# An encoder trunk's MLP: up projection as seven block products, weight sums on GpSimd, down products added to the residual

## The chip, the cores and the metric

The kernel runs on one core of a Trainium2 chip. The metric is the device time of one execution in microseconds (us); of several runs the median is given. Five engines work beside each other, each on its own queue of instructions in a fixed order: TensorE (PE in the profile; its weight loads are shown apart as PEld), VectorE (DVE), ScalarE (ACT), GpSimd (POOL) and SyncE (SP), which here issues the loads of weights. TensorE reads from SBUF and writes to PSUM; all other engines work element by element. A tile framework puts the instructions in order and inserts the waits.

## What is computed

Two layers over 512 tokens of width 1024, in float32. Each layer has three mixing branches, then an MLP of width 4096:

```python
for l in range(DEPTH):
    ...                                  # three branches, gates, w_out
    x = x + merged @ w_out[l]
    hn = rms_norm(x, ln2[l])
    x = x + jnp.square(jax.nn.relu(hn @ w_up[l])) @ w_down[l]
return rms_norm(x, final_norm)
```

The MLP is where the change lies: `w_up[l]` is 1024 x 4096, `w_down[l]` 4096 x 1024. The row scale of the norm, r, is left out ahead of the MLP and comes in behind it as r squared, since relu and square let it pass.

## The kernel before

**Precision.** Every large product is made of three matmuls on a rounded high part and the rest, the low part: high x high, high x low, low x high. Weights arrive in chunks of 128x1024 (512 KB). `wsplit` (L205) makes the two parts of a chunk: ScalarE casts the high part `wh` (L207), DVE subtracts to get the low part `wl` (L208). There are three buffers of each (WB). `split` (L259) does the same with activations, on ScalarE (L262) and DVE (L263).

**Stages of a layer.** The G stage (tiles tA to gC) makes most of the input projection, then come the branches, then `yA`, `wo` (output projection into the residual `xr`, eight tiles of 128 tokens x 512), then the MLP. `norm_tok` (L306) turns `xr` for the next projection: transposes on TensorE, scale on ScalarE, low part on DVE.

**MLP.** It goes by four quarters (`qd`) of the 4096 hidden columns. In each, eight up projections (`proj`, L216, called at L1166): a chunk holds a block of 128 hidden columns over all 1024 inputs, and 8 x 3 matmuls with 512 tokens moving fill one bank of PSUM (L212 to L214). ScalarE applies relu and square (L1171, L1172). `left_first` and `left_second` (L358, L366) make block sums and differences of the result (`sf`) and their two parts (`sh`).

**Seven products.** The down projection multiplies 2x2 blocks with seven products in place of eight. `seven` (L407) does that: it needs sums of the four weight blocks b11, b12, b22, b21. `early_sums` (L400) makes t1 = b11 + b12 and then b12 + b22; two more are made ahead of product 6 and product 4 (L431, L433). All four sorts are DVE additions of 128x1024, two chunks each. Products are taken in the order 1, 2, 6, 7, 5, 4, 3; each has 24 matmuls of 512 columns and its result is added in `on`: in the first three quarters into eight tiles `acc` (copied by ScalarE where they are first written, L466, added by DVE, L468), in the last quarter scaled by r squared (`r2`, `nr2`) into `xr` (L462), after `acc` itself was added there (L473). `done` then writes `xr` to DRAM (`xspill`) or finishes the output.

**Order.** The framework orders each engine's queue; `hp()` marks urgent instructions. Weight chunks are loaded into ten buffers `wq` (NQ) for the seven products, or two buffers `wr` (WR) for the rest. GpSimd issues the loads and stores of intermediate values through DRAM, and does a few small operations.

## Time and profile before

| | us |
|---|---|
| median of 3 runs (lowest, highest) | 1730.45 (1729.51, 1731.83) |
| span of the profiled execution | 1729.5 |
| PE busy | 1685.3 |
| PEld busy | 1405.0 |
| DVE busy | 1297.1 |
| ACT busy | 1017.1 |
| POOL busy | 146.1 |

The profile gives the span from the first to the last instruction of one execution; that execution's own time is not listed apart from the three runs. Rows of groups read: line, engine, operation, tiles written and read, shapes, count, then busy us and mean ns of one, then the idle time in front. Rows by stretch give, for each engine, the busy us and the number of instructions. Rows in order of time give start and duration in us; `x2` marks two in a row, merged. The two MLPs run from about 528.6 to 861 us and from 1386.8 to 1724 us.

### The profile page before, as it was taken

The page shows a single profiled execution, that of the slowest core. Times are in us where ns is not written, and L with a number is a line of the kernel's source. Part 1 is how long each engine was busy: PE and PEld are TensorE (multiplying, and loading weights), DVE is VectorE, ACT ScalarE, POOL GpSimd, SP SyncE. Part 2 cuts the span into 40 slices and gives each one's busy share as a digit, 9 for nine tenths or more (in the row PEclk, how much of TensorE's full clock was granted, in tenths as well). Part 3 has the DMA queues.
Part 4 walks back from the last instruction along what each step waited for, and adds up shares of the span by engine and source line. Part 5 has one row for each costly group of instructions (what it writes and reads, how often), then busy time and mean ns, then how long its engine had stood idle before and what let it go on. Part 6 is the DMA issues. An engine that isn't in the chain of part 4 may idle for free.

```text
span 1729.5 us, 21976 instructions
## 1 busy us (share of the span) xinstructions
PE 1685.3 (97%) x8024; PEld 1405.0 (81%) x8024; DVE 1297.1 (75%) x2009; ACT 1017.1 (59%) x1715; POOL 146.1 (8%) x215
## 2 busy tenths in 40 slices
PE   8999999999999999999999999999999999999997
PEld 7888878887877888888888787888877878888886
DVE  7996977687566668686889869876776567686867
ACT  7665567677335555545665754877772355545454
POOL 0011200000310000000010112000004000000001
PEclk9999999999999999999999999999999999999999
DMA  8342232231545332233423422322317353232311
GB/s 331 98 146 92 83 104 81 72 104 55 203 187 182 98 110 98 98 98 98 134 92 126 147 93 71 104 79 75 111 48 273 130 182 98 98 98 97 119 65 49
DMA packets 58283, 200.04 MB, mean 116 GB/s; under 512 B 7904, under 2 KB 8288, under 8 KB 58176
## 3 DMA queue, kind: packets, MB, share of 16 engines
q1 hardware_dynamic: 44640, 154.72, 26.6%
q0 software_dynamic: 13248, 43.40, 6.7%
q8 instruction: 63, 1.03, 0.3%
q10 hardware_dynamic: 288, 0.52, 0.1%
q14 instruction: 44, 0.36, 0.1%
HBM read 177.64 MB, written 20.97 MB: 115 GB/s over the span
## 4 chain that ended last, share of the span: by engine, by line
PE 43%; issue 20%; DVE 4%; ACT 2%; POOL 0%; POOLq 0%; ACTq 0%; DVEq 0%
PE up L213 3%; PE up L212 3%; PE up L214 3%; PE dA L418 2%; PE dA L420 2%; PE dA L419 2%; PE at L558 1%; PE gA L418 1%; PE gz L214 1%; PE gz L213 1%; PE gz L212 1%; PE dC L418 1%; PE dC L420 1%; PE dC L419 1%; PE gA L420 1%
## 5 line engine op out<-in xcount | busy, mean ns | idle before, releaser
L207 ACT CAST wh<-wq 128x1024 fp32r<-128x1024 f32 x201 | 211.4, 1052 | 208.2 <-PE up L213 49.3
L208 DVE TENSOR_TENSOR wl<-wq,wh 128x1024 fp32r<-128x1024 f32 x201 | 245.1, 1222 | 117.1 <-ACT wh L207 116.1
L208 DVE TENSOR_TENSOR wl<-wr,wh 128x1024 fp32r<-128x1024 f32 x166 | 203.9, 1228 | 148.0 <-ACT wh L207 147.6
L207 ACT CAST wh<-wr 128x1024 fp32r<-128x1024 f32 x166 | 174.0, 1049 | 214.6 <-PE up L213 67.3
L212 PE MATMUL up<-xh,wh 128*128 128x512 f32 x512 | 199.2, 390 | 1.9 <-ACT u L1171 1.9
L213 PE MATMUL up<-xl,wh 128*128 128x512 f32 x512 | 200.6, 392 | 0.1
L214 PE MATMUL up<-xh,wl 128*128 128x512 f32 x512 | 199.1, 391 | 0.0
L212 PEld LDWEIGHTS up<-xh,wh 128*128 128x128 f32 x512 | 96.3, 188 | 22.7 <-ACT u L1171 2.7
L213 PEld LDWEIGHTS up<-xl,wh 128*128 128x128 f32 x512 | 96.4, 188 | 20.3 <-DVE xl L266 0.6
L214 PEld LDWEIGHTS up<-xh,wl 128*128 128x128 f32 x512 | 96.5, 189 | 19.8
L418 PE MATMUL dA<-wh,sh 128*128 128x512 f32 x256 | 99.8, 390 | 0.0
L419 PE MATMUL dA<-wh,sh 128*128 128x512 f32 x256 | 99.7, 389 | 0.0
L420 PE MATMUL dA<-wl,sh 128*128 128x512 f32 x256 | 92.6, 390 | 0.0
L600 DVE TENSOR_TENSOR ex<-ex 128x512 f32<-128x512 f32 x112 | 78.1, 715 | 6.3 <-ACT kt L575 5.4
L558 PEld LDWEIGHTS at<-qt,kt 128*128 128x128 f32 x448 | 57.0, 191 | 9.9 <-ACT kt L575 4.7
L558 PE MATMUL at<-qt,kt 128*128 128x128 f32 x448 | 59.6, 276 | 5.6 <-DVE qt L573 2.7
L572 ACT ACTIVATE qt<-ex 128x512 f32<-128x512 f32 x56 | 37.7, 674 | 46.3 <-DVE ex L600 38.5
L274 POOL TENSOR_TENSOR rs<-ms,mhalf_t 128x4 f32<-128x4 f32 (+2 forms) x15 | 17.3, 1156 | 530.6 <-DVE ms L272 527.5
L420 PEld LDWEIGHTS dA<-wl,sh 128*128 128x128 f32 x256 | 48.1, 188 | 10.0
L418 PEld LDWEIGHTS dA<-wh,sh 128*128 128x128 f32 x256 | 48.1, 188 | 10.0
L419 PEld LDWEIGHTS dA<-wh,sh 128*128 128x128 f32 x256 | 48.1, 188 | 9.9
L262 ACT CAST sh<-sf 128x512 fp32r<-128x512 f32 x64 | 39.7, 621 | 24.3 <-DVE sf L383 18.0
(403 smaller groups left out, 4403.0 us busy)
## 6 DMA issues: line engine op xcount, KB each, us to landing
wr<-in_ws_dram SPq DMA_DIRECT2D x166, 512.0 KB, 3.3
wq<-in_ws_dram SPq DMA_DIRECT2D x117, 512.0 KB, 4.3
thd<-zt POOLq DMA_DIRECT2D x32, 256.0 KB, 2.5
th<-thd POOLq DMA_DIRECT2D x32, 256.0 KB, 4.6
mgd<-mg POOLq DMA_DIRECT2D x16, 256.0 KB, 2.9
mcd<-th POOLq DMA_DIRECT2D x16, 256.0 KB, 2.5
mC<-mcd POOLq DMA_DIRECT2D x16, 256.0 KB, 6.7
mB<-mgd POOLq DMA_DIRECT2D x16, 256.0 KB, 6.6
```

What stands on the lines that cost most here:

```text
L207: nc.scalar.copy(hi, raw)
L208: nc.vector.tensor_tensor(lo, raw, hi.bitcast(F32), ALU.subtract)
L212: nc.tensor.matmul(pt, whi, xhi, start=first, stop=False)
L213: nc.tensor.matmul(pt, whi, xlo, start=False, stop=False)
L214: nc.tensor.matmul(pt, wlo, xhi, start=False, stop=last)
L262: nc.scalar.copy(hi, src)
L418: nc.tensor.matmul(pt, xh[:, t], hi[:, c], start=start and k == 0, stop=False, skip_group_check=True)
L419: nc.tensor.matmul(pt, xl[:, t], hi[:, c], start=False, stop=False, skip_group_check=True)
L420: nc.tensor.matmul(pt, xh[:, t], lo[:, c], start=False, stop=k == 3, skip_group_check=True)
L558: nc.tensor.matmul(pt[:, c], kk(st), qq[:, c], start=True, stop=True)
L572: nc.scalar.activation(qt.rearrange(shp, b=nb, h=2), e_q, AF.Exp)
L600: nc.vector.tensor_tensor(o_ap, o_ap, ap_of(ex, i_, [[istep, 2]] + z), ALU.add)
```

## The change

Four things are changed together.

The up projection is made of seven block products too. `up_unit` does half a quarter: 512 hidden columns in four 256-wide block columns and rows, over 512 tokens in two halves, so 256 tokens move in each matmul and a product has 24 matmuls. Its left side, the sums of the normed activations, is made once a layer in `norm_move` (`turn` and `sums`, with `left_sums`). Its result comes out already in the blocks that the down projection needs, and the parts for down are made product by product. `left_first` and `left_second` are gone.

The four sorts of weight sums are made by GpSimd (`eng`) in the up and the down projection, and `early_sums` there also in the G stage, except at a layer's first `uload`.

The down products of all four quarters are scaled and added straight to `xr`; `acc` is gone.

Buffers: eleven `wq`, 26 `h`, `sf` in another pool, and a scratch of 4096 bytes for the DMAs that GpSimd issues.

```diff
         for qd in range(4):
-            res += [(l, "up", qd, f) for f in range(8)]
+            res += [(l, "up", qd, j, q) for j in range(2) for q in range(4)]
...
-             "h": 22}
+             "h": 26}
...
-    WR, WB, NZ, NCT, NSM, NQ = 2, 3, 3, 4, 3, 10
+    WR, WB, NZ, NCT, NSM, NQ = 2, 3, 3, 4, 3, 11
...
+    def upload(l, qd, j):
+        first = (qd, j) == (0, 0)
+        raw = [None] * 4
+        for q in (0, 3, 1, 2) if first else range(4):
+            raw[q] = [WRAW() if first and q in (0, 3) else WQ()]
+            with hp():
+                nc.sync.dma_start(raw[q][0], ws[CHUNK[(l, "up", qd, j, q)]])
+        return raw + [[WQ() if first else WRAW()]]
...
-    def early_sums(raw):
+    def early_sums(raw, eng):
         b11, b12, b22, b21, t1 = raw
-        for i in range(2):
-            nc.vector.tensor_tensor(t1[i], b11[i], b12[i], ALU.add)
...
+        for i in range(len(t1)):
+            eng.tensor_tensor(t1[i], b11[i], b12[i], ALU.add)
+        for i in range(len(t1)):
+            eng.tensor_tensor(b12[i], b12[i], b22[i], ALU.add)
...
                     if n == 6:
-                        V.tensor_tensor(b11[i], t1[i], b22[i], ALU.add)
+                        (eng or V).tensor_tensor(b11[i], t1[i], b22[i], ALU.add)
                     elif n == 4:
-                        V.tensor_tensor(b21[i], b21[i], b11[i], ALU.add)
+                        (eng or V).tensor_tensor(b21[i], b21[i], b11[i], ALU.add)
...
+    def up_unit(raw, hx, new):
+        b11, t3, b22, b21, t1 = [t[0] for t in raw]
...
+        use = {1: ("m", b11), 2: ("a", b21), 6: ("m", b11), 7: ("s", t3), 5: ("m", t1), 4: ("s", b21), 3: ("m", b22)}
...
+            if n == 1:
+                A.copy(a11, v)
+            elif n == 2:
+                V.tensor_tensor(a11, a11, v, ALU.add)
+                square(a11)
+                put(1, a11)
+            elif n == 6:
+                A.copy(a21, v)
+            elif n == 7:
+                A.activation(a22, v, AF.Copy, scale=-1.0)
+            elif n == 5:
+                V.tensor_tensor(a22, a22, v, ALU.subtract)
+                square(a22)
+                put(4, a22)
+            elif n == 4:
+                V.tensor_tensor(a21, a21, v, ALU.add)
+                square(a21)
+                sa0, sa1 = SF(), SF()
+                V.tensor_tensor(sa0, a22, a21, ALU.subtract)
+                V.scalar_tensor_tensor(sa1, sa0, -1.0, a11, ALU.mult, ALU.subtract)
+                put(6, sa1)
+                put(5, sa0)
+                sb0 = SF()
+                V.tensor_tensor(sb0, a11, a21, ALU.subtract)
+                put(7, sb0)
...
+            else:
+                A.activation(a12, v, AF.Relu, scale=-1.0)
+                A.activation(a12, a12, AF.Square)
+                put(2, a12)
+                sb1 = SF()
+                V.scalar_tensor_tensor(sb1, a12, -1.0, h.pop("s"), ALU.mult, ALU.subtract)
+                put(3, sb1)
+        for n in (1, 2, 6, 7, 5, 4, 3):
...
+                if n == 6:
+                    G.tensor_tensor(b11, t1, b22, ALU.add)
+                elif n == 4:
+                    G.tensor_tensor(b21, b21, b11, ALU.add)
+                hi, lo = wsplit(w)
+            for f in range(2):
+                o = pt[:, f * HT:(f + 1) * HT]
+                for k in range(4):
+                    c = slice(k * HT + f * P, k * HT + (f + 1) * P)
+                    xh, xl = hx[k][n]
+                    nc.tensor.matmul(o, hi[:, c], xh, start=start and f == 0 and k == 0, stop=False, skip_group_check=True)
+                    nc.tensor.matmul(o, hi[:, c], xl, start=False, stop=False, skip_group_check=True)
+                    nc.tensor.matmul(o, lo[:, c], xh, start=False, stop=k == 3, skip_group_check=True)
...
-    def down(qd, raw, hs, acc, xr, r2, nr2, done, last):
+    def down(qd, raw, hs, xr, r2, nr2, done, last):
...
+            r = r2 if sign > 0 else nr2
+            V.scalar_tensor_tensor(xr[t][fl], pt, r[:, t:t + 1], xr[t][fl], ALU.mult, ALU.add)
...
+        seven(raw, hs, "d", on, apart=last and qd == 3, eng=nc.gpsimd)
...
-                early_sums(nxt)
+                early_sums(nxt, nc.gpsimd)
...
-        n2 = norm_tok("ln2", l, xr, False)
+        n2 = norm_move(l, xr)
...
             with hp():
-                n2.turn(fl, range(4), "s" if fl else "c")
+                n2.turn(fl)
         with hp():
             n2.end()
+            n2.sums()
...
+        raw = upload(l, 0, 0)
+        early_sums(raw, nc.gpsimd)
         for qd in range(4):
...
+            for j in range(2):
+                nxt = upload(l, qd, 1) if j == 0 else uload(l, "dn", qd, t1=WRAW)
+                hs += up_unit(raw, n2.hx, new)
+                early_sums(nxt, nc.gpsimd)
+                raw = nxt
...
+            else:
+                nxt = upload(l, qd + 1, 0)
+            down(qd, raw, hs, xr, r2, nr2, done, last)
...
-    nc = _bacc.Bacc("TRN2", target_bir_lowering=False, num_devices=1)
+    nc = _bacc.Bacc("TRN2", target_bir_lowering=False, num_devices=1, dynamic_dma_scratch_size=4096)
```

In `norm_move`, `turn` transposes `xr` as before, copies and scales it on ScalarE into `xf` (kept in float32), and makes the two parts; `sums` calls `left_sums` for four pairs of these tiles: four DVE operations of 256 columns and two splits of 512 each.

How the instructions stand shows three places. First, DVE where layer 0 goes from `wo` to the MLP, before: behind the last additions to `xr` (L1108) come the norm (L339, L272, with L1115 waiting for GpSimd's power), then weight sums of the first down projection (L403) and low parts of the turned tiles (L266).

```order
L1108 SCALAR_TENSOR_TENSOR xr_4442<-wo_4675,xr_4442 128x512
L208 TENSOR_TENSOR wl_4980<-wr_4977,wh_4979 128x1024
L339 TENSOR_TENSOR s_1062_4844<-ss_981_4451 128x4
L272 TENSOR_SCALAR ms_4846<-s_1062_4844 128x4
L1115 TENSOR_TENSOR r_1065_4850<-rs_4848 128x4
L1117 TENSOR_SCALAR r_1066_4852<-r_1065_4850 128x4
L403 TENSOR_TENSOR wq_4919<-wq_4903,wq_4907 128x1024
L266 SCALAR_TENSOR_TENSOR xl_4809<-xT_4810,vec_t,xh_4808 128x512
```

And now, on the same engine from the same place: the sums of the activations (`sf`, `xs`) stand between the norm and the low part for product 6 (`wl_5020`); of the four tiles the first and the last are shown in part.

```order
L1220 TENSOR_TENSOR r_1093_4918<-rs_4860 128x4
L1222 TENSOR_SCALAR r_1094_4920<-r_1093_4918 128x4
L383 TENSOR_TENSOR sf_4864<-xf_4817,xf_4641 128x256
L384 SCALAR_TENSOR_TENSOR sf_4864<-sf_4864,xf_4641 128x256
L387 SCALAR_TENSOR_TENSOR sf_4862<-xf_4817,sf_4864 128x256
L279 TENSOR_TENSOR xl_4820<-xf_4817,xh_4819 128x512
...
L279 TENSOR_TENSOR sh_5015<-u_4930,sh_5014 128x512
L279 TENSOR_TENSOR xs_4910<-sf_4906,xs_4909 128x512
L279 TENSOR_TENSOR xs_4915<-sf_4904,xs_4914 128x512
L224 TENSOR_TENSOR wl_5020<-wr_4932,wh_5019 128x1024
```

The low part of product 6's weight is now the thirtieth instruction behind the norm's last.

Second, GpSimd from the same norm on, before: behind the power (L274) it has nothing but the stores of the residual, which come in the last quarter.

```order
L1075 DMA mB_4547<-mgd 128x512
L1075 DMA mB_4559<-mgd 128x512
L274 TENSOR_TENSOR rs_4848<-ms_4846,mhalf_t 128x4
L1147 DMA xspill<-xr_4435 128x512
L1147 DMA xspill<-xr_4437 128x512
```

And now, further on in the same stretch, from the down sums of the first quarter (L432, L434 in `seven`) into those of the second quarter's two units (L404, L406 in `early_sums`, L551, L553 in `up_unit`):

```order
L432 TENSOR_TENSOR wq_5205<-wr_5221,wq_5213 128x1024
L432 TENSOR_TENSOR wq_5207<-wr_5222,wq_5215 128x1024
L434 TENSOR_TENSOR wq_5217<-wq_5217,wq_5205 128x1024
L434 TENSOR_TENSOR wq_5219<-wq_5219,wq_5207 128x1024
L404 TENSOR_TENSOR wr_5486<-wq_5478,wq_5480 128x1024
L404 TENSOR_TENSOR wr_5745<-wq_5737,wq_5739 128x1024
L406 TENSOR_TENSOR wq_5480<-wq_5480,wq_5482 128x1024
L406 TENSOR_TENSOR wq_5739<-wq_5739,wq_5741 128x1024
L551 TENSOR_TENSOR wq_5478<-wr_5486,wq_5482 128x1024
L553 TENSOR_TENSOR wq_5484<-wq_5484,wq_5478 128x1024
```

64 sums of 128x1024 stand in that queue in each MLP; a unit's sums stand behind the first sum of the unit after it.

Third, DVE inside the up projection of the second quarter, before: low parts of weights (L208), and sums and low parts of the results (L382 to L386, L263).

```order
L382 TENSOR_TENSOR sf_5583<-u_4862 128x256
L383 SCALAR_TENSOR_TENSOR sf_5583<-sf_5583,u_4862 128x256
L263 TENSOR_TENSOR sh_5580<-u_4862,sh_5579 128x512
L386 SCALAR_TENSOR_TENSOR sf_5544<-u_4862,sf_5583 128x256
L263 TENSOR_TENSOR sh_5587<-sf_5583,sh_5586 128x512
L263 TENSOR_TENSOR sh_5592<-sf_5544,sh_5591 128x512
L208 TENSOR_TENSOR wl_5727<-wr_5724,wh_5726 128x1024
```

And now, on the same engine: the additions from PSUM (L512, L520, L524) stand between low parts of weights (L224) that belong to later products.

```order
L512 TENSOR_TENSOR u_4930<-u_4930,up_5776 128x2x256
L224 TENSOR_TENSOR wl_5873<-wr_5486,wh_5872 128x1024
L279 TENSOR_TENSOR sh_5809<-u_4930,sh_5808 128x512
L224 TENSOR_TENSOR wl_5909<-wq_5484,wh_5908 128x1024
L224 TENSOR_TENSOR wl_5958<-wq_5482,wh_5957 128x1024
L520 TENSOR_TENSOR u_4930<-u_4930,up_5746 128x2x256
L224 TENSOR_TENSOR wl_6019<-wq_5737,wh_6018 128x1024
L524 TENSOR_TENSOR u_4930<-u_4930,up_5842 128x2x256
```

DVE's reading of product 5 (L520) now stands behind the weights of the unit's last two products.

More of the change, by code (lines that the diff above doesn't have):

```diff
@@ L398, in left_x, with seven @@
         return res
[L400 removed]
+    def early_sums(raw, eng):
         b11, b12, b22, b21, t1 = raw
[L402 to L407 removed]
+        for i in range(len(t1)):
+            eng.tensor_tensor(t1[i], b11[i], b12[i], ALU.add)
+        for i in range(len(t1)):
+            eng.tensor_tensor(b12[i], b12[i], b22[i], ALU.add)
+    def seven(raw, hs, name, on, order=(1, 2, 6, 7, 5, 4, 3), between=None, apart=False, eng=None):
         b11, t3, b22, b21, t1 = raw
@@ L1126, in trunk @@
         n1 = norm_tok("ln1", l + 1, xr, True)
-        acc = [[T("tv", "acc"), T("tv", "acc")] for _ in range(4)]
         fn_t = []
@@ L1185, in trunk @@
                     nxt = uload(l + 1, "un", 0)
-            down(qd, raw, hs, acc, xr, r2, nr2, done, last)
+            else:
+                nxt = upload(l, qd + 1, 0)
+            down(qd, raw, hs, xr, r2, nr2, done, last)
+            if qd < 3:
+                early_sums(nxt, nc.gpsimd)
+                raw = nxt
         if not last:
@@ L1190, in trunk @@
             raw = nxt
-            early_sums(raw)
+            early_sums(raw, nc.vector)
             end("mlp")
```

134 lines of the change are left out of this document (73 added, 61 removed).

## The prediction

> **What bounds the kernel now.** I read the page's first part, then busy time by stretch for one quarter of the MLP (up projection, then down), then the instructions of TensorE in order of time.
>
> ```profile
> span 1729.5 us, 21976 instructions
> PE 1685.3 (97%) x8024; PEld 1405.0 (81%) x8024; DVE 1297.1 (75%) x2009; ACT 1017.1 (59%) x1715; POOL 146.1 (8%) x215
> ...
> core 0: us, PE busy (x) PEld busy (x) DVE busy (x) ACT busy (x) POOL busy (x), PEclk, DMA share, GB/s
> 616.20:659.80 43.60, 43.60 (x194) 36.13 (x193) 24.92 (x37) 24.11 (x37) 0.00 (x0) 1.00 0.28 95
> 659.80:697.80 38.00, 38.00 (x170) 31.47 (x169) 32.90 (x38) 17.66 (x19) 0.00 (x0) 1.00 0.35 113
> ```
>
> TensorE never rests in a quarter: 43.6 us up, 38.0 us down, 81.6 us together, at full clock. DVE is busy for 57.8 of the 81.6 us, GpSimd not at all. So before the change only TensorE work counts, and DVE has 24 us per quarter to spare. Eight quarters (four in each layer) make 653 us of the span. The span is within 0.1 us of the fastest of the three runs (1729.51), so nothing worth counting lies around it; their median, 1730.45, is 1.0 above.
>
> **The matmuls.** What does one matmul cost in a stream, with 512 columns moving and with 256?
>
> ```profile
> 528.58 0.39 PE L212 MATMUL up<-xh,wh 128*128 128x512 f32 x1
> 528.81 0.39 PE L213 MATMUL up<-xl,wh 128*128 128x512 f32 x1
> 529.03 0.39 PE L214 MATMUL up<-xh,wl 128*128 128x512 f32 x1
> ...
> 1276.79 0.28 PE L964 MATMUL sc<-kl,q 128*128 128x256 f32 x1
> 1276.91 0.39 PE L254 MATMUL yC<-wh,yh 128*128 128x512 f32 x1
> ...
> 1276.67 0.19 PEld L964 LDWEIGHTS sc<-kl,q 128*128 128x128 f32 x1
> 1276.79 0.19 PEld L254 LDWEIGHTS yC<-wh,yh 128*128 128x128 f32 x1
> ```
>
> Durations (0.39) overlap; the cost is from start to start: 0.227 us at 512 columns (43.6 / 192 in the up stretch). At 256 columns the attention scores show 0.12, and weight loads follow each other at 0.12 too, though each lasts 0.19. I take 0.117, between half of 0.227 (0.1135) and 0.12. The up projection goes from 1536 matmuls x 0.227 = 348.7 us to 16 units x 168 = 2688 x 0.117 = 314.5: TensorE alone gains 34 us (26 at 0.12, 44 at 0.1135). A unit (half a quarter's up projection) takes 19.7 us, a quarter 39.3 + 38.0 = 77.3.
>
> **DVE's own work.** Back to back, DVE instructions overlap by about 0.08 us:
>
> ```profile
> 673.25 2.35 DVE L208 TENSOR_TENSOR wl<-wq,wh 128x1024 fp32r<-128x1024 f32 x2
> L208 DVE TENSOR_TENSOR wl<-wq,wh 128x1024 fp32r<-128x1024 f32 x201 | 245.1, 1222 | 117.1 <-ACT wh L207 116.1
> 672.06 1.28 DVE L468 TENSOR_TENSOR acc<-acc,dB 128x512 f32<-128x512 f32 x2
> L462 DVE SCALAR_TENSOR_TENSOR xr<-dA,r,xr x16: 742/746/752, 829.5 to 1720.5; 128x512 f32<-128x512 f32 x16
> ```
>
> So a weight's low part costs 2.35 - 1.22 = 1.13 to 1.14, a 512-wide operation 1.28 - 0.68 = 0.60, and the scaled add into the residual 0.746 - 0.08 = 0.66. Per unit after the change: 7 low parts (8.0) and 14 operations of 512 (three from PSUM, four block sums, seven low parts of activations: 8.4), 16.4 us. Down: 14 low parts (15.9) and 14 scaled adds (9.3), 25.2; the eight ScalarE copies of the first quarter become such adds, and the eight preparatory adds of the last vanish, 5 us each way. A quarter: 2 x 16.4 + 25.2 = 58.0 us, as much as now (57.8), but no longer with the weight sums in it, and crowded into the up projection: 32.8 of 39.3 us. ScalarE gets 7 casts and 18 operations of 512 a unit:
>
> ```profile
> L207 ACT CAST wh<-wq 128x1024 fp32r<-128x1024 f32 x201 | 211.4, 1052 | 208.2 <-PE up L213 49.3
> L262 ACT CAST sh<-sf 128x512 fp32r<-128x512 f32 x64 | 39.7, 621 | 24.3 <-DVE sf L383 18.0
> ```
>
> 7 x 1.05 + 18 x 0.62 = 18.5, under the unit's 19.7: hidden behind TensorE, barely.
>
> **The sums on GpSimd.** The trace holds no 1024-wide sum there, but it holds 512-wide ones, and what DVE does meanwhile (three places, DVE and GpSimd):
>
> ```profile
> 1059.95 2.17 POOL L918 TENSOR_TENSOR cq<-cq,cos 128x512 f32<-128x512 f32 x1 [5.13 <-DVE sh L916]
> 1059.76 1.21 DVE L208 TENSOR_TENSOR wl<-wr,wh 128x1024 fp32r<-128x1024 f32 x1
> 1060.88 1.78 DVE L600 TENSOR_TENSOR ex<-ex 128x512 f32<-128x512 f32 x1
> ...
> 333.54 1.53 POOL L582 TENSOR_TENSOR dg<-key 128x512 f32<-128x512 f32 x1 [5.61 <-PE oT L655]
> 333.83 2.31 DVE L208 TENSOR_TENSOR wl<-wr,wh 128x1024 fp32r<-128x1024 f32 x1
> ...
> 1032.50 1.28 POOL L582 TENSOR_TENSOR dg<-key 128x512 f32<-128x512 f32 x1 [1.56 <-ACT key L580]
> 1032.24 0.69 DVE L708 TENSOR_TENSOR ck<-ck,rb 128x512 f32<-128x512 f32 x1
> 1032.84 1.48 DVE L877 SCALAR_TENSOR_TENSOR bu<-yb,bu 128x512 f32<-128x512 f32 x1
> ```
>
> First place: GpSimd starts while wl runs, gets nowhere until wl ends at 1060.97, and is over at 1062.12; the next DVE operation, normally 0.69, takes 1.78. Second: wl, normally 1.22, takes 2.31. Each time DVE loses 1.09 us to one GpSimd operation. Third: the addition ck reads one input from PSUM and one from SBUF, and neither side is slowed; only bu, with both inputs in SBUF, waits until 1033.64. So a two-input GpSimd operation and a DVE operation with two SBUF inputs exclude each other, and GpSimd gets in at the next end of a DVE instruction. A 1024-wide sum should shut DVE out for 2 x 1.09 = 2.18 us; it can't be under 1.09, nor over twice the whole undisturbed instruction, 2.56. I take 2.18, since the 512 elements scale it. On DVE itself such a sum costs 1.14. By the Trainium skill, page "GPSIMD Engine Reference", section "3.1 Elementwise — side-by-side cycle accounting", 2048 elements measured 4497 ns, so 2.25 us for a sum; with that my sum would come out 9 us higher. Its page "SBUF — State Buffer", section "Who interferes with whom", says that the loser blocks for the whole instruction; here the loss was 1.09 of 1.28, and by the rule the sum would be about 49 us higher (8 x 16 x 0.38).
>
> A quarter has 4 sums in each unit and 8 for down: 16 x 2.18 = 34.9 us. DVE and GpSimd one after the other need 58.0 + 34.9 = 92.9 us; even if every PSUM operation slips under a sum, the 45.2 us of two-SBUF work (58.0 less 6 x 0.60 and 14 x 0.66) plus 34.9 is 80.1, over TensorE's 77.3. DVE with GpSimd becomes the bound.
>
> By stage: the sums of units wait for loads and freed buffers, so I put about nine in the up stretch, seven in down. Down: 25.2 + 15.3, less three pairs of adds under sums (4.0), is 36.5, and TensorE's 38.0 holds. Up: 32.8 + 19.6 - 0.6 = 51.8. Together 89.8; were the work free to move over the stage border, five pairs of adds and a single one or two could hide (7.5), which gives 92.9 - 7.5 = 85.4. Three buffers for split weights allow a little of that: I take 88, nearer the first. 8 x (88 - 81.6) = **+51 us**, TensorE's 34 us of gain swallowed in it.
>
> **Start of the MLP.** The block sums of the activations (left_sums over four tiles) now stand ahead of product 6.
>
> ```profile
> 527.42 2.05 DVE L1108 SCALAR_TENSOR_TENSOR xr<-wo,xr 128x512 f32<-128x512 f32 x3
> 532.88 0.16 DVE L1115 TENSOR_TENSOR r<-rs 128x4 f32<-128x4 f32 x1 [1.16 <-POOL rs L274]
> PE xT L327 <- DVE xl L266: 2.3, 1, 2.3
> PE up L212 <- ACT u L1171: 0.9, 1, 0.9
> L382 DVE TENSOR_TENSOR sf<-u 128x256 f32<-128x256 f32 x32 | 13.6, 426 | 0.0
> ```
>
> TensorE starts on up at 528.58 and stalls 3.2 us today. DVE passes the norm at 533.25 (532.88 and two small ones), 4.7 after that start. Then stand 15 operations of 256 (at 0.426 - 0.08 = 0.34: 5.1), 14 of 512 (8.4) and the low part of product 6's weight (1.1): 14.6 us, so product 6 starts at 19.3 or later, while transposes (1.8) and two products (24 x 0.117 each) cover 7.4. On DVE, the bound from here, 4.7 us of waiting and 12.3 us of new work (14.6 less three operations that the unit's 16.4 holds already), less two weights split ahead (2.3), are 14.7; with a last product after its last weight (4 us) that makes 18 to 19, against 3.2: about +14 a layer, **+28**. The sums' hold-ups here are in the 16.
>
> **The rest.** Outside the MLP eight weight sums a layer leave DVE in the G stage. Each holds DVE for 2.18 instead of 1.14, and in layer 0 DVE has little room:
>
> ```profile
> 41.00:86.00 45.00, 44.90 (x203) 37.01 (x201) 43.02 (x50) 30.86 (x40) 0.00 (x0) 1.00 0.30 97
> 86.00:128.00 42.00, 41.90 (x191) 34.61 (x192) 39.61 (x54) 28.22 (x38) 7.21 (x12) 1.00 0.44 144
> mB<-mgd POOLq DMA_DIRECT2D x16, 256.0 KB, 6.6
> ```
>
> 82.6 of 87 us; 8 x 1.04 = 8.3 more would overrun by 4, and operations from PSUM hide most: **+1** (0 to +8). The smaller scratch for GpSimd's DMAs I cost at 0: it still issues the same loads, such as mB (6.6 us to land), well ahead; up to +6 if issues must wait. Weight bytes are the same.
>
> Sum: 1729.5 + 51 + 28 + 1 = **1810 us**, 4.6% over the median.
>
> **Rivals.**
> - TensorE stays the bound (the sums fall where DVE rests or reads PSUM). A quarter is 77.3, 8 x -4.3 = -34; at the start product 6 still waits, 12 us a layer against 3.2, +18: 1713, faster. For it: GpSimd was idle in these stretches. Against: all three places above, and 80.1 > 77.3. It decides where a quarter falls under 78 us (81.6 less an eighth of the 28): a sum then holds DVE for 2.05 us at most with all PSUM work hidden, or 0.9 by my split of the stages. 13%.
> - Sums fully serial, and GpSimd's queue or DVE waits for a product at its head: 92.9 a quarter is 8 x 11.3 = +90, with 28 and 8 around: 1856; 2 us of such waits in each of 16 units: 1888. 17%.
> - Evenly spread sums: 80.1 a quarter, -12 + 28 + 1: 1746, up to 1765. 8%.
> - Weight loads don't keep up (0.188 each): 2688 x 0.188 = 505 us, +156, so near 1900. Against: PEld's starts 0.12 apart. 2%.
> - The first two mix to no change: 2%.
>
> My forecast has the remaining 58% (1765 to 1855).
>
> **How the numbers follow.** 1728 leaves about 13% below (the first rival), 1870 leaves 7% above. A run of this kernel tells 0.2% (3.5 us) from no change. Faster 0.13, same 0.04, slower 0.83.
>
> **What would show it.** Right: up matmuls with 256 columns 0.114 to 0.12 apart inside a product; GpSimd sums of 2.3 us and more; wl low parts of 3.4 us beside them; TensorE under 85% busy in up stretches, waiting for wl; quarters of 85 to 92 us; a stall of over 12 us before the third product of a layer. Wrong: wl stays at 1.22 beside sums, or quarters near 77 us; then the exclusion doesn't carry over to these sums, or the order hides it, and the kernel is faster.

## The result, and the profile after

The changed kernel takes 1871.45 us (median of four runs, 1870.58 to 1872.41), the kernel before 1729.98 beside it on the same chip: a ratio of 1.081, 95% interval 1.0794 to 1.0827. It is 141 us slower. The forecast had the sign and 80 us; 61 us are missing in it, and the time lies 1.5 us above the range. Times are medians of a run's executions; one of the four of run 10 took 4798 us and is left out, so what later expectations call the run at 1767 stands here with 1765.5 us.

The page's first part of the changed kernel's profile:

```profile
span 1868.9 us, 24699 instructions
PE 1719.8 (92%) x9176; PEld 1472.5 (79%) x9176; DVE 1526.6 (82%) x1993; ACT 1086.6 (58%) x1811; POOL 545.6 (29%) x359
```

TensorE's share falls from 97 to 92%, DVE's busy time grows by 230 us, GpSimd's by 400. Where the time lies is seen in busy time by stretch. The rows are the MLP's first quarter in layer 0 (from the end of the output projection), then the up and the down projection (up and down for short) of the second quarter, a steady one; the columns are those of the prediction's first fence.

```profile
531.10:652.30 121.20, 89.84 (x523) 79.43 (x522) 104.10 (x102) 59.58 (x86) 58.80 (x22) 0.87 0.31 109
652.30:697.10 44.80, 42.26 (x338) 41.85 (x337) 41.12 (x34) 29.66 (x42) 22.47 (x9) 0.96 0.28 95
697.10:744.60 47.50, 42.99 (x170) 34.10 (x169) 43.22 (x38) 18.95 (x23) 21.07 (x9) 0.89 0.27 89
```

A quarter takes 92.3 us (before: 81.6), and in it DVE is busy for 84.3. TensorE waits in both halves, and its granted clock (PEclk) is 0.96 and 0.89 where it was 1.00. The first quarter takes 121.2 us against 87.6.

What holds DVE, seen at the end of up and the start of down: rows of DVE, then GpSimd, then TensorE. (Line numbers are the changed kernel's: L224 low part of a weight, L279 low part of an activation, L527 to L532 sums of relu-squared blocks, L574 scaled add to the residual, L404 to L406 `early_sums`, L432 and L434 late sums of down, L551 and L553 of up, L419 to L421 matmuls of down, L560 to L562 of up.)

```profile
687.35 3.42 DVE L224 TENSOR_TENSOR wl<-wq,wh 128x1024 fp32r<-128x1024 f32 x1
695.73 2.16 DVE L279 TENSOR_TENSOR sh<-u,sh 128x512 fp32r<-128x512 f32 x1 [0.28 <-ACT sh L278]
699.66 2.77 DVE L528 SCALAR_TENSOR_TENSOR sf<-sf,u 128x512 f32<-128x512 f32 x1
703.49 3.47 DVE L279 TENSOR_TENSOR sh<-sf,sh 128x512 fp32r<-128x512 f32 x2
708.74 1.40 DVE L574 SCALAR_TENSOR_TENSOR xr<-dA,r,xr 128x512 f32<-128x512 f32 x2
...
686.96 2.74 POOL L406 TENSOR_TENSOR wq<-wq,wq 128x1024 f32<-128x1024 f32 x1
694.93 2.41 POOL L432 TENSOR_TENSOR wq<-wr,wq 128x1024 f32<-128x1024 f32 x1 [5.24 <-DVE wl L224]
699.10 2.78 POOL L432 TENSOR_TENSOR wq<-wr,wq 128x1024 f32<-128x1024 f32 x1 [1.76 <-DVE wl L224]
703.70 2.71 POOL L434 TENSOR_TENSOR wq<-wq,wq 128x1024 f32<-128x1024 f32 x1 [1.82 <-DVE wl L224]
...
702.27 0.39 PE L421 MATMUL dA<-wl,sh 128*128 128x512 f32 x1
705.35 0.39 PE L421 MATMUL dB<-wl,sh 128*128 128x512 f32 x1
709.63 0.77 PE L419 MATMUL dA<-wh,sh 128*128 128x512 f32 x1 [3.90 <-DVE xr L574]
```

Four sums on GpSimd, four DVE operations that are held, that is, take longer because a sum runs beside them: a low part takes 3.42 us in place of 1.21, then 512-wide operations 2.16, 2.77 and 2.79 (3.47 less 0.68) in place of 0.68. Behind them in DVE's queue stands the scaled add of P1: its matmuls were done at about 702.7, it runs at 708.74. The third product needs P1's PSUM bank, and TensorE rests 3.90 us. In the chain of waits by engine:

```profile
PE up L560 <- ACT wh L223: 50.3, 10, 17.5
PE dA L419 <- DVE xr L574: 30.1, 8, 3.9
```

The largest single wait, 17.5 us, is the forecast's stall before the third product of a layer, 542.3 to 559.8.

Marks between stages, from the starts and ends of TensorE's matmuls, turn the profiles' 139.4 us into terms: 2 x 22.6 = 45 at the start of the MLP (first quarter less a steady one: 29.2 against 6.6, mean of two layers), 8 x 10.5 = 84 in quarters (92.1 against 81.6, mean of five), 10.5 outside (2.4 up to the MLP of layer 0, 9.2 from the last product of layer 0 to the MLP of layer 1, and 1.2 less at the end). Against the forecast's 51, 28 and 1 that is 33 more in quarters, 17 at the start and 9.5 outside.

### The profile page after: what moved, and what is told of

Its sections match the earlier page's. It is cut to its first block, busy times and chain, and to the rows that moved or that the text cites. A ratio compares the mean times of both kernels' runs of the same rounds, so it can differ in the third digit from the quotient of the medians.

```text
span 1868.9 us, 24699 instructions
## 1 busy us (share of the span) xinstructions
PE 1719.8 (92%) x9176; PEld 1472.5 (79%) x9176; DVE 1526.6 (82%) x1993; ACT 1086.6 (58%) x1811; POOL 545.6 (29%) x359
## 5 line engine op out<-in xcount | busy, mean ns | idle before, releaser
L224 DVE TENSOR_TENSOR wl<-wq,wh 128x1024 fp32r<-128x1024 f32 x275 | 424.1, 1551 | 69.5 <-ACT wh L223 66.8
L223 ACT CAST wh<-wq 128x1024 fp32r<-128x1024 f32 x275 | 287.6, 1049 | 235.8 <-PE dA L420 47.3
L224 DVE TENSOR_TENSOR wl<-wr,wh 128x1024 fp32r<-128x1024 f32 x140 | 187.2, 1338 | 81.8 <-ACT wh L223 81.5
L560 PE MATMUL up<-xs,wh 128*128 128x256 f32 x512 | 154.2, 302 | 55.5 <-ACT wh L223 50.3
L560 PEld LDWEIGHTS up<-xs,wh 128*128 128x128 f32 x512 | 105.5, 206 | 59.7 <-ACT wh L223 52.4
L562 PE MATMUL up<-xs,wl 128*128 128x256 f32 x512 | 149.2, 296 | 3.0 <-DVE wl L224 3.0
L561 PE MATMUL up<-xs,wh 128*128 128x256 f32 x512 | 151.2, 296 | 0.0
L419 PE MATMUL dA<-wh,sh 128*128 128x512 f32 x256 | 110.2, 430 | 30.1 <-DVE xr L574 30.1
L404 POOL TENSOR_TENSOR wr<-wq,wq 128x1024 f32<-128x1024 f32 x30 | 78.6, 2621 | 174.9 <-DVE wl L224 174.7
L406 POOL TENSOR_TENSOR wq<-wq,wq 128x1024 f32<-128x1024 f32 x40 | 122.0, 3058 | 4.3 <-DMA wq<-in_ws_dram 3.0
L562 PEld LDWEIGHTS up<-xs,wl 128*128 128x128 f32 x512 | 104.1, 205 | 3.6 <-DVE wl L224 3.6
L561 PEld LDWEIGHTS up<-xs,wh 128*128 128x128 f32 x512 | 105.6, 206 | 0.0
L421 PE MATMUL dA<-wl,sh 128*128 128x512 f32 x256 | 98.8, 422 | 7.1 <-DVE wl L224 7.1
L279 DVE TENSOR_TENSOR sh<-u,sh 128x512 fp32r<-128x512 f32 x48 | 82.8, 1725 | 8.1 <-ACT sh L278 7.8
L419 PEld LDWEIGHTS dA<-wh,sh 128*128 128x128 f32 x256 | 53.6, 209 | 44.6 <-ACT wh L223 33.3
L704 DVE TENSOR_TENSOR ex<-ex 128x512 f32<-128x512 f32 x112 | 78.1, 715 | 6.3 <-ACT kt L679 5.6
L562 PE MATMUL up<-xh,wl 128*128 128x256 f32 x256 | 73.8, 288 | 3.9 <-DVE wl L224 3.8
L561 PE MATMUL up<-xl,wh 128*128 128x256 f32 x256 | 73.9, 289 | 1.4 <-DVE xl L279 1.4
```

The lines of the kernel that those rows point to most:

```text
L223: nc.scalar.copy(hi, raw)
L224: nc.vector.tensor_tensor(lo, raw, hi.bitcast(F32), ALU.subtract)
L279: nc.vector.tensor_tensor(lo, src, hi.bitcast(F32), ALU.subtract)
L404: eng.tensor_tensor(t1[i], b11[i], b12[i], ALU.add)
L406: eng.tensor_tensor(b12[i], b12[i], b22[i], ALU.add)
L419: nc.tensor.matmul(pt, xh[:, t], hi[:, c], start=start and k == 0, stop=False, skip_group_check=True)
```

## The experiments

**1. All MLP sums on DVE.**

```diff
-                    G.tensor_tensor(b11, t1, b22, ALU.add)
+                    V.tensor_tensor(b11, t1, b22, ALU.add)
...
-                early_sums(nxt, nc.gpsimd)
+                early_sums(nxt, nc.vector)
```

> The changed kernel with all block sums of MLP weights back on DVE (sixteen a quarter); everything else as changed. Theory A (DVE and GpSimd shut each other out, 2.2 us for each sum, and DVE works its queue in order): the hold goes, DVE's work becomes 63.4 + 16 x 1.14 = 81.6 us a quarter with a few us of idle time, so quarters of 82 to 87 against 92.3, and 1790 to 1825 us. Rival B (the loss comes from the seven products of the up projection themselves, their evictions and their activation sums, wherever weight sums are made): DVE only gets more work, quarters stay at 92 or grow, 1865 us or more.

Measured: 1780.1 us, 1.028 times before (1.0261 to 1.0298), 91 less than the changed kernel. Busy time of a quarter:

```profile
640.50:721.70 81.20, 79.56 (x505) 71.80 (x504) 77.28 (x87) 48.90 (x64) 0.00 (x0) 1.00 0.32 104
```

This is theory A, though 10 us under the range that was given for it. The quarter is 81.2 (mean of five: 81.7), DVE's busy time 77.3 with no operation beyond its usual length. The same sixteen sums cost 16.1 us of DVE (77.3 less the 61.2 of the next run, 1.0 each), and the quarter is 10 us shorter than with them on the engine that had been idle.

**2. No MLP sums.**

```diff
-                if n == 6:
-                    G.tensor_tensor(b11, t1, b22, ALU.add)
-                elif n == 4:
-                    G.tensor_tensor(b21, b21, b11, ALU.add)
...
-        raw = upload(l, 0, 0)
-        early_sums(raw, nc.gpsimd)
+        raw = upload(l, 0, 0)
```

> The changed kernel without any block sum of MLP weights: the products of up and down use a raw block in place of each sum (seven products, splits, evictions and loads as before; the sums are left out). Theory A: DVE's 63.4 us a quarter and its idle time fit under TensorE's 77.3, so quarters of 77 to 80, 8 x -13.5 = -108, and at the start two sums less in the chain: 1745 to 1770 us. Rival B: quarters stay over 85, so over 1810 us.

Measured: 1739.0 us, ratio 1.0048 (1.0030 to 1.0066). Up and down of a quarter:

```profile
627.10:667.40 40.30, 40.30 (x338) 40.30 (x337) 30.30 (x36) 30.44 (x43) 0.00 (x0) 1.00 0.31 105
667.40:705.50 38.10, 38.10 (x170) 31.53 (x169) 30.88 (x36) 18.57 (x22) 0.00 (x0) 1.00 0.33 111
```

Now TensorE is the bound: 78.4 us a quarter, 336 matmuls of 256 columns in 40.3, so 0.12 each. The time is 6 us under theory A's range. The sums are 132 of the 141 us. And even without them the kernel isn't faster: TensorE's gain of 8 x 3.2 = 26 us is there, but the start takes 10.3 us more a layer than before, and some 10 us are lost outside the MLP, where the G stage's sums are still on GpSimd.

**3. The kernel before, with its down sums on GpSimd.**

```diff
-                    early_sums(raw)
+                    early_sums(raw, nc.gpsimd)
...
-        seven(raw, hs, "d", on, apart=last and qd == 3)
+        seven(raw, hs, "d", on, apart=last and qd == 3, eng=nc.gpsimd)
```

> The kernel before, with its sums of down weights (eight a quarter, no others) on GpSimd; up projection and accumulation as before. Theory A by DVE's busy time alone: 57.8 - 8 x 1.14 + 8 x 2.2 = 66.3 of 81.6 us, so no change (within 0.3% of 1730). Rival C (what counts is that a sum on GpSimd comes late, 2 x 2.35 us in a chain ahead of a product, with DVE's queue standing behind it): 2 to 4 us a quarter, 1745 to 1765 us.

Measured: 1746.6 us, ratio 1.0083 (1.0066 to 1.0100): in rival C's range, but not by its account. Steady quarters take 82.9, 1.3 more than before and not 2 to 4, although eight DVE operations are held in each, for 13.4 to 14.8 us: DVE still rests for 19.5 (first row). The rest comes in the last quarter of each layer (91.8 and 89.2 against 83.5 and 81.6); the first quarters are 2.8 and 3.9 us shorter.

```profile
650.20:733.00 82.80, 82.27 (x361) 67.28 (x360) 63.28 (x69) 40.80 (x55) 22.29 (x8) 1.00 0.30 102
...
PE up L214 <- DVE wl L208: 9.1, 2, 4.6
```

Where a last quarter begins, DVE adds `acc` to `xr` (L473, operations with two SBUF inputs). Sums hold two of these and two low parts, 7.4 us in all, and TensorE waits 4.6 us for one of the low parts (second row: two such waits in the run), behind which its granted clock is 0.50 for some 4 us. Over the whole quarter DVE rests for 19 us and more there too. So a hold costs little as long as TensorE needs nothing that stands behind it.

**4. Early loads at the start.** In the changed kernel the first loads into `wq` are issued late: rows of SP's and GpSimd's queues.

```profile
550.16 2.98 SPq L214 DMA_DIRECT2D wq<-in_ws_dram  x6
...
553.93 2.34 POOL L404 TENSOR_TENSOR wq<-wr,wq 128x1024 f32<-128x1024 f32 x1 [19.57 <-DMA wq<-in_ws_dram]
```

SyncE's own wait is for the last of the activations' sums (L387):

```profile
SPq L214 <- DVE sf L387: 34.3, 1, 34.3
```

The buffers lie over the pool whose tiles `xf` these sums read until 550. With the tiles `yi` in a pool of their own under the buffers, the loads need not wait for that:

```diff
-    ... "Y2": ("yi", "th", "mg"), ...
+    ... "Yi": ("yi",), "Y2": ("th", "mg"), ...
...
+        begin("Yi")
         begin("Y2")
```

> The changed kernel with the tiles of the output projection's inputs in a pool of their own below the tiles that hold the normalised activations, so that the first weight loads of the MLP no longer wait for the block sums of the activations. Theory (the start is late because those loads are issued only at 550 us and two GpSimd sums follow them): loads at about 530 us, the third product 7 to 10 us earlier in each layer, 1851 to 1858 us. Rival (DVE's fifteen small sums and what else stands on DVE set the start): within 3 us of 1871.

Measured: 1869.4 us, ratio 1.0798 (1.0778 to 1.0818): no gain, the theory fell. The trace says why (GpSimd, then DVE, same stretch):

```profile
536.20 2.36 POOL L404 TENSOR_TENSOR wq<-wr,wq 128x1024 f32<-128x1024 f32 x1 [0.66 <-PE up L562]
538.64 2.41 POOL L551 TENSOR_TENSOR wr<-wq,wq 128x1024 f32<-128x1024 f32 x1
541.01 2.52 POOL L406 TENSOR_TENSOR wq<-wq,wq 128x1024 f32<-128x1024 f32 x1
...
536.34 2.50 DVE L383 TENSOR_TENSOR sf<-xf,xf 128x256 f32<-128x256 f32 x1 [0.40 <-ACT xf L466]
538.87 2.45 DVE L384 SCALAR_TENSOR_TENSOR sf<-sf,xf 128x256 f32<-128x256 f32 x1
541.36 2.45 DVE L387 SCALAR_TENSOR_TENSOR sf<-xf,sf 128x256 f32<-128x256 f32 x1
```

The sums came 18 us earlier and fell on DVE's sums of the activations: operations of 0.42 us take 2.5, one after the other. In TensorE's rows the third product now starts at 551.7 instead of 559.8, but it gets its operands piece by piece and ends at 568.1, in the changed kernel at 566.4.

**5 and 6. Which sums are dear.** On GpSimd only the sums for up, then only those for down (the others on DVE):

```diff
-                early_sums(nxt, nc.gpsimd)
+                early_sums(nxt, nc.gpsimd if j == 0 else nc.vector)
...
-        seven(raw, hs, "d", on, apart=last and qd == 3, eng=nc.gpsimd)
+        seven(raw, hs, "d", on, apart=last and qd == 3, eng=nc.vector)
```

> The changed kernel with the eight sums for down on DVE and the eight of the two units of up on GpSimd in each quarter. If each sum on GpSimd costs the same wherever it stands, half of the 11 us between 92.3 and 81.3 comes back: quarters of 86 to 87.5 and 1822 to 1840 us. If the sums beside down are the dear ones (their hold stands ahead of the scaled adds that free PSUM banks), most comes back here: quarters of 82 to 85, 1790 to 1815 us. By the stage split of the forecast (up bound by DVE, down by TensorE) little comes back: over 1845 us.

> The reverse: the sums of up on DVE, the eight for down on GpSimd. Same cost everywhere: quarters of 86 to 87.5, 1822 to 1835 us. Dear beside down: quarters of 88 to 91, over 1840 us. By the stage split of the forecast: quarters of 82 to 84, under 1805 us.

Measured: 1791.5 us (1.0347, 1.0330 to 1.0365) and 1833.3 us (1.0595, 1.0573 to 1.0616). A quarter of each:

```profile
645.90:728.60 82.70, 80.95 (x506) 73.33 (x505) 77.21 (x79) 48.66 (x64) 23.59 (x9) 0.98 0.31 102
...
643.40:731.20 87.80, 81.59 (x506) 72.71 (x505) 81.69 (x79) 49.08 (x64) 21.79 (x8) 0.98 0.29 96
```

By the mean of five quarters, up's sums cost 0.2 us more on GpSimd than on DVE (81.9 against 81.7), down's 6.8 (88.5). The other 10 us or so of run 5 over run 1 lie in the first quarters. The stage split of the forecast had it the other way round. Run 6 has the quarters that were expected if down's sums are the dear ones, but its time is 7 us under the one given with them. With up's sums on GpSimd, seven DVE operations are held in a steady quarter, for 9.2 to 9.7 us, little more than the 8 us that the sums take on DVE itself; with down's, eight for 13.1, at the end of a unit, where nearly every operation of DVE reads two SBUF inputs and P1's add stands behind them.

**7. GpSimd busy, but reading nothing.**

```diff
+    def fake(x):
+        nc.gpsimd.memset(x, 0.01)
+        nc.gpsimd.memset(x, 0.02)
+        nc.gpsimd.memset(x[:, 0:S], 0.01)
...
-                    G.tensor_tensor(b11, t1, b22, ALU.add)
+                    fake(b11)
```

> The changed kernel with each sum of MLP weights on GpSimd replaced by three fills of the same tile with a constant (1024, 1024 and 512 wide, by the trace's 0.52 us for 512 about 2.4 us together): GpSimd is busy as long, at the same places of its queue, with the same tiles behind it, but reads nothing from SBUF. Sums are left out with it. Theory A (the exclusion of two-input operations is what costs): wl stays at 1.22 us beside the fills, quarters of 78 to 81, 1740 to 1770 us. Rival C (it is the lateness of a 2.35 us GpSimd step ahead of products): quarters of 88 to 92, over 1830 us.

Measured: 1744.2 us, ratio 1.0076 (1.0059 to 1.0093). Busy time of a quarter, then the low parts of weights as a group here and in the changed kernel:

```profile
631.50:709.90 78.40, 78.40 (x506) 71.83 (x505) 60.78 (x71) 48.88 (x64) 37.99 (x49) 1.00 0.33 108
...
L224 DVE TENSOR_TENSOR wl<-wq,wh 128x1024 fp32r<-128x1024 f32 x275 | 349.3, 1273 | 143.6 <-ACT wh L223 139.1
```

```profile
L224 DVE TENSOR_TENSOR wl<-wq,wh 128x1024 fp32r<-128x1024 f32 x275 | 424.1, 1551 | 69.5 <-ACT wh L223 66.8 <-DMA xt<-in_xt_dram 0.2 <-PE gC L421 0.2
```

GpSimd works 38 us of each quarter at the same places, and the quarter stays at 78.4: its lateness costs 5 us in the whole kernel, against 132 for the sums. So the exclusion is shown, not only argued: what costs is that GpSimd reads SBUF beside DVE, and not that it is busy or late. (A fill also waits for no input; no run takes that apart, but the low parts' usual length beside fills doesn't hang on it.) The Trainium skill, page "SBUF — State Buffer", section "Who interferes with whom", says that a DVE instruction with two SBUF inputs contends with a GpSimd instruction that reads SBUF and not with one that only writes there; the two runs agree with it.

**8. The G stage's sums on DVE too** (on top of run 1).

```diff
-                early_sums(nxt, nc.gpsimd)
+                early_sums(nxt, nc.vector)
```

> The changed kernel with all block sums of weights on DVE, those of the G stage too. Against the run with only the MLP's sums on DVE (1780) it prices the G stage's eight sums a layer on GpSimd. If they cost what the traces show up to the output projection (2.4 to 3.7 us a layer and a few more at the layers' border): 1768 to 1775 us. By the forecast (+1 in all): 1778 to 1781 us.

Measured: 1771.0 us (1.0231, 1.0213 to 1.0249), 9 less than run 1: the G stage's sixteen sums cost 9 us, not 1.

**9. Sums by DMA.** Each sum as an adding transfer, with `yi` in its own pool and the G stage's sums on DVE.

```diff
+    def add_to(x, y):
+        nc.gpsimd.dma_start(x, y, accum_op=ALU.add)
...
-                    G.tensor_tensor(b11, t1, b22, ALU.add)
+                    add_to(b11, t3)
```

> The changed kernel with every block sum of MLP weights made by a DMA that adds one tile to another on its way (issued by GpSimd; the first sum of each set starts from a second load of its block), the G stage's sums back on DVE, and the output projection's inputs in a pool of their own below the normalised activations' tiles. Neither DVE nor GpSimd's arithmetic makes sums then. If the transfers keep up: quarters of 78.4 as without sums, the start without weight sums in its chain (4 to 5 us earlier a layer than in the run without sums, whose first loads waited for the activations' sums) and 9 us less in the G stage: 1739 - 9 - 9 = 1721, 1715 to 1735 us. If they are late (16 of them in a quarter, 20% to twice the DMA share now): quarters over 82, over 1760 us.

Measured: 1853.4 us, ratio 1.0708 (1.0693 to 1.0722): the sums come late. DVE has only 39 us to do in 60 (last row below), but the DMA engines are busy for 0.83 of the time, and an addition lands 4.9 or 7.2 us after its issue in the median:

```profile
wq<-wq POOLq DMA_DIRECT2D x94, 512.0 KB, 4.9
wr<-wq POOLq DMA_DIRECT2D x32, 512.0 KB, 7.2
...
700.00:760.00 60.00, 55.20 (x302) 48.91 (x302) 39.12 (x45) 27.00 (x34) 8.62 (x10) 0.94 0.83 213
```

**10. Early loads without GpSimd's sums:** run 8 with the pool of run 4.

> The kernel with all weight sums on DVE (1771 us) and, besides, the output projection's inputs in a pool of their own, so that the MLP's first loads do not wait for the activations' sums. With GpSimd's sums gone nothing shuts DVE out at the start, so earlier loads should now be worth what they were not beside GpSimd: 2 to 5 us a layer, 1761 to 1767 us. If DVE's queue (its own weight sums stand among the activations' sums) is the bound there: within 3 us of 1771.

Measured: 1765.5 us (1.0202, 1.0185 to 1.0218), 5 less than run 8; the first quarters are 3.0 and 2.4 us shorter. The early loads that were worth nothing beside GpSimd's sums are worth something here.

**11. P1 evicted by ScalarE.**

```diff
+            if which == "P1":
+                d = SF().rearrange("p a b -> p (a b)")
+                nc.scalar.activation(d, pt, AF.Copy, scale=r[:, t:t + 1])
+                V.tensor_tensor(xr[t][fl], xr[t][fl], d, ALU.add)
```

> The changed kernel with the first down product (P1) evicted by ScalarE into SBUF and added to the residual by DVE from there; all sums on GpSimd as changed. If down is slow because P1's eviction stands in DVE's queue behind operations that GpSimd's sums hold, and the third product waits for its PSUM bank (30 us of such waits in the changed kernel's trace): that wait goes, quarters of 88 to 90.5, 1845 to 1860 us. If the bank is only one of several things that DVE is late for (its work and the holds set the pace anyway, and the new additions from SBUF can be held too): within 5 us of 1871, or slower.

Measured: 1882.4 us, ratio 1.0874 (1.0859 to 1.0889), slower by 11. The bank's wait (dA, 30.1 us) is gone, and 56 us of new ones have come, at the next thing that DVE is late for (ScalarE's cast in the first row waits itself for DVE's sums of blocks):

```profile
PE dB L419 <- ACT sh L278: 31.0, 8, 4.1
PE dB L420 <- DVE sh L279: 25.0, 8, 3.4
```

So the bank was a symptom: DVE's queue sets the pace of down.

**12 and 14. Half of the sums, or a quarter of them, by DMA,** the others on DVE (on top of run 10; shown is run 12, in run 14 the first of these stays on DVE).

```diff
+            nc.gpsimd.dma_start(t1[i], b12[i], accum_op=ALU.add)
...
+            nc.gpsimd.dma_start(b12[i], b22[i], accum_op=ALU.add)
...
+                    V.tensor_tensor(b11, b11, t3, ALU.add)
```

> The run at 1767 (all weight sums on DVE, output projection's inputs in their own pool) with the early half of the MLP's sums (the two that stand ahead of a set's first product: b11 + b12, from a second load of b11, and b12 + b22) made by accumulating DMAs, and the late half (ahead of products 6 and 4) on DVE. DVE's work falls to 61.2 + 8 x 1.02 = 69.4 us a quarter. If the eight DMAs a quarter land ahead of need (with sixteen, 0.73 to 0.83 of the DMA engines' time was busy and products waited): quarters of 78.4 to 79.5, 8 x -3 = -24, and 3 to 5 us a layer at the start: 1732 to 1742 us, perhaps under the kernel before. If they are late: quarters over 82, over 1767 us.

> The run at 1767 with one sum in four (b12 + b22) made by an accumulating DMA, the other three on DVE. DVE's work is 61.2 + 12 x 1.02 = 73.4 us a quarter, plus 4 us of idle time as in the run with all sums on DVE: 77.4, just under TensorE's 78.4. Expected: quarters of 78.5 to 80, 1738 to 1752 us. If DMA latency (5 to 7 us an addition) counts: 1760 us or more.

Measured: 1802.1 us (1.0417, 1.0394 to 1.0439) and 1794.0 us (1.0372, 1.0356 to 1.0387); quarters of 86.1 and 85.4. They miss their expectations by 60 and 42 us, and both are slower than run 10. DVE has less to do (73.6 of 86 us busy in run 14, 78.1 of 82 in run 10) and yet TensorE waits longer: for low parts in down 17.1 us in eight waits, in run 10 1.6 us in one. Behind short gaps its clock falls (last section). In run 14 the low part that TensorE waits for at 692.9 stands in a stretch in which DVE doesn't rest (681.5 to 696.7 us), behind a rest of 2.9 us in up; why the order came out so, with fewer sums in the queue, stays open.

**13. No sums of the activations** (on top of run 10).

```diff
+        if 1 in h and new.__name__ == "new":
+            h.update({5: h[1], 6: h[2], 7: h[4], 3: h[1]})
+            return
```

> The run at 1767 (all weight sums on DVE, output projection's inputs in their own pool) without the block sums of the MLP's activations: products 3, 5, 6 and 7 of up use raw blocks of the activations in place of the sums (left out). If these sums (15 subtractions of 256 columns a layer less one, and 16 low parts of 512) set the start, as the forecast had it: 10 to 14 us a layer, 1739 to 1747 us. If the weight sums and splits at the start are as much in the way: 4 to 7 us a layer, 1753 to 1759 us.

Measured: 1739.0 us (1.0047, 1.0031 to 1.0064), 26.5 less than run 10. The first quarters are 12.6 and 14.2 us shorter, steady ones the same.

**15. TensorE kept busy in its gaps.**

```diff
+            if n == 2:
+                keep = PT("c", "warm")
+                for _ in range(14):
+                    nc.tensor.matmul(keep[:, 0:HT], lo[:, 0:P], hx[0][2][0], start=True, stop=True)
...
+                if n == 2 and s_ == 0 and eng:
+                    keep = PT("s", "warm")
+                    for _ in range(15):
+                        nc.tensor.matmul(keep, hs[1][n][0][:, 0:P], split_w[0][1][:, 0:S], start=True, stop=True)
```

> The changed kernel with extra matmuls, whose result nobody reads, where TensorE stands idle in each quarter: 14 of 256 columns (1.7 us) after the second product of each unit of up, 15 of 512 columns (3.4 us) after the first half of the second product of down. In the changed kernel a quarter's TensorE time is 78.4 us at full clock, 7.1 idle (the longest gaps 1.9 and 3.9 us) and 6.8 lost at half clock behind the gaps. If the half clock is part of the cost (DVE itself rests 3.1 us in that phase, waiting for TensorE): quarters of 85.5 to 89.5, 1825 to 1850 us. If DVE's queue sets the time whatever TensorE's clock is: within 5 us of 1871, or slower by the matmuls that outlast the gaps.

Measured: 1858.3 us, ratio 1.0739 (1.0725 to 1.0754), 13 less than the changed kernel. A quarter:

```profile
640.00:730.50 90.50, 86.54 (x549) 78.03 (x548) 84.80 (x71) 48.77 (x65) 43.39 (x17) 1.00 0.29 94
```

The clock is 1.00 throughout this quarter, and it is 1.8 us shorter, between the two expectations (3 to 7 us, and none). The half clock is a cause of its own, but a small one; DVE's 84.8 us stay.

No version beat the kernel before.

## Why the prediction was right and wrong

- *Sign and mechanism, right.* GpSimd's two-input sums and DVE's operations with two SBUF inputs exclude each other also at 1024 elements (runs 1, 2, 7); TensorE's quarter without that was put at 77.3 and is 78.4.
- *Hold of one sum, right in size; of all sums, too long.* A low part beside a sum takes 3.42 us, so 2.21 of hold (forecast 2.18; a sum that nothing disturbs takes 2.34 to 2.41). Of the sixteen sums of a steady quarter fifteen hold a DVE operation, most for less than their length: 25.2 us, where the forecast's 88 holds 30.0 (34.9 less what hides). Two of the fifteen are L528 in the two units; it is held every time, and only a run without these sums on GpSimd shows its usual length (changed kernel, then run 7):

```profile
L528 DVE SCALAR_TENSOR_TENSOR sf<-sf,u 128x512 f32<-128x512 f32 x16 | 44.4, 2772 | 0.6
L540 DVE SCALAR_TENSOR_TENSOR sf<-sf,u 128x512 f32<-128x512 f32 x16 | 11.1, 692 | 0.5
```

- *The step "a quarter: 58.0 us" held.* DVE's own work is its busy time less the holds, 84.3 - 25.2 = 59.1 us in the second quarter (61.2 in run 2, where DVE waits for TensorE and fewer of its operations stand back to back). The 63.4 us in the expectations of runs 1 and 2 are too many by the holds of L528 (twice 2.1), which is a part of why run 1 came out under its range.
- *The step "by stage" failed.* It put up at 51.8 (32.8 us of own work, 19.0 of holds), and down, with 25.2 and 11.3, under TensorE's 38.0. Measured are 44.8 and 47.5. The holds are shared out nearly as forecast (eight in up, 14.2 us; seven in down, 11.0). DVE's own work isn't: about 26.9 us of it are done in up's stretch and 32.2 in down's, since a unit's last operations are still to be done when TensorE is already at down. The adds from PSUM stand behind these operations, which the sums for down hold, and TensorE waits for the first add. So TensorE's 38.0 doesn't cover down. Run 5 against 6 (+0.2 and +6.8 a quarter) shows which sums are dear.
- *Idle time of DVE, which the forecast put at nothing, failed too.* DVE works its queue in order, and its waits add up to 8.0 us of a quarter (3.9 even in run 1). 59.1 + 25.2 + 8.0 = 92.3. Against the 88 of the forecast, own work is 1.1 more, idle time 8.0 more, the holds 4.8 less; that the last two partly cancel is luck. So the term is +84, not +51: near the second rival's 92.9, whose makeup (no hold hidden, no idle time) wasn't the real one either.
- *The start, +28 forecast, +45 measured.* The step that priced the activations' sums at 14 us a layer was right in size: run 13 measures 12.6 and 14.2. (Its own terms, 18 to 19 less 3.2, give 15 to 16.) The path was another. In the forecast the third product waits for its low part in DVE's queue, 19.3 us after the first; in the changed kernel it waits for loads whose buffers these sums keep until 550, and then for two sums on GpSimd, and starts 28.8 us after the first. The sentence "the sums' hold-ups here are in the 16" failed: by first quarter less steady one, mean of two layers, late loads add 3.0 (25.5 in run 8, 22.5 in run 10), sums on GpSimd rather than DVE 3.7 (29.2 against 25.5), and 2.8 are left for weight sums and splits on DVE (9.4 in run 13 against 6.6 before). With 13.1 for the activations' sums (22.5 against 9.4) that is 22.6 a layer. The shares hold for this order of steps: with the sums on GpSimd, early loads gained nothing (run 4).
- *The G stage, +1 forecast (0 to 8), 9 measured* (run 8 against 1). It shows clearly only between the MLPs: from layer 0's last product to the MLP of layer 1 the changed kernel takes 532.8 us and run 1 531.6, run 8 525.0, the kernel before 523.6. Up to the MLP of layer 0 the 2.4 us are too few to be read: runs 10 and 14 do the same work there and take 528.1 and 532.0.
- *The DMA's scratch at 0* wasn't tried by itself; run 10, which has it, takes 528.1 us up to the MLP of layer 0 (before: 528.6) and 524.4 between the MLPs (523.6), so no loss shows.
- *Of the signs listed:* matmuls 0.12 apart, sums over 2.3, low parts of 3.4 and the stall over 12 us came; TensorE under 85% in up didn't (42.26 of 44.80, 94%), since down took more of the loss; quarters are at the upper edge of 85 to 92 (92.1).

## What to carry to other kernels

Work handed to an idle GpSimd isn't free for DVE: a sum that costs DVE 1.0 us of its own time cost it 1.6 us of holds on GpSimd, and 4 us of idle time a quarter came on top, so look at what DVE runs at that very place, and count operations with two SBUF inputs. Price a queue that works in order by what stands behind the held instruction, not by the share of busy time: eight holds of 13 us in all cost 1.3 us in a steady quarter of the kernel before and 6.8 in the changed one. And check whether the gain survives with the disputed cost removed altogether: with free sums the seven products gave 26 us in quarters and gave 21 back at the start, and some 10 more were lost outside the MLP.

## What the runs showed of the hardware

TensorE's clock halved behind some short rests. Windows of the changed kernel (TensorE's busy time, granted clock, DMA share, GB/s) around the 3.9 us wait in down:

```profile
797.00:799.00 2.00, 1.08 (x5) 1.00 0.00 0
799.00:801.00 2.00, 0.00 (x0) 0.96 0.00 0
801.00:803.00 2.00, 1.02 (x3) 0.50 0.00 0
...
808.00:811.00 3.00, 3.00 (x8) 0.50 0.60 203
811.00:814.00 3.00, 3.00 (x14) 0.99 0.55 164
```

The clock is at a half for about 10 us, and matmuls of 512 columns come 0.43 us apart. The Trainium skill, page "TensorE: Matmul & The Clock Gate", Part 1, names one idle window of about 3.4 us as what brings the half clock. This rest is longer than that, but the clock had fallen by 801, less than 3 us after the rest began. In run 14 a shorter rest was enough: TensorE rested 2.1 us, and the clock fell behind it, within 3 us of its beginning; the measurement decides here.

```profile
693.00:695.00 2.00, 0.00 (x0) 1.00 0.01 4
695.00:697.00 2.00, 1.97 (x6) 0.66 0.41 111
697.00:699.00 2.00, 2.00 (x7) 0.50 0.92 301
699.00:701.00 2.00, 2.00 (x10) 0.99 0.28 113
```

The length of the rest alone doesn't decide it. In run 10 TensorE rests once in a steady quarter, for 1.5 us; behind one of these rests the clock stayed at 1.00, behind another it was at a half for about 3 us (a quarter each; TensorE's busy time, granted clock, DMA share, GB/s):

```profile
713.20:794.40 81.20, 79.56 (x499) 0.98 0.32 104
632.00:713.20 81.20, 79.56 (x507) 1.00 0.32 104
```

By TensorE's rows 6.8 us of a quarter of the changed kernel were lost to the half clock (85.2 us busy, 78.4 in run 2); filling the gaps gave back 1.8.
